# Moving a few VectorE and ScalarE instructions within the pair phases of a macaron transformer block

## The chip, the cores and the metric

The kernel runs on one core of a Trainium2 chip. The metric is the device time of one launch in microseconds (us). TensorE (PE in the profile, PEld for its weight loads) multiplies, VectorE (DVE) and ScalarE (ACT) prepare operands and empty its banks, GpSimd (POOL) and SyncE (SP) issue transfers. Each engine works through its own list in order; semaphores tie the lists together.

## The reference

A block of 512 positions by 1024 features in float32: half a SwiGLU layer, a token mixer, half a SwiGLU layer, a norm.

```python
def swiglu(x, w_gate, w_up, w_down):
    return (jax.nn.silu(x @ w_gate) * (x @ w_up)) @ w_down

x = x + 0.5 * swiglu(rmsnorm(x, ffn1_norm[layer]), ...)
x = x + token_mixer(rmsnorm(x, mix_norm[layer]), ...)
x = x + 0.5 * swiglu(rmsnorm(x, ffn2_norm[layer]), ...)
return rmsnorm(x, final_norm)
```

The hidden width of a SwiGLU layer is 2816, that is 22 tiles of 128.

## The kernel before, in words

**Products in two parts.** Every float32 operand is split into a high part (a rounding cast, by ScalarE) and a low part (operand minus high part, by VectorE). A product is then three matmuls into one PSUM bank: high by high, high by low, low by high (`mm3`, L124 to L126).

**Plain and pair phases.** In each SwiGLU layer (function `ffn`, called with the suffix "a" for the first and "b" for the second) some hidden tiles are computed plainly with matmuls 512 wide. The rest go in pairs of hidden tiles by a scheme of Strassen's kind, with seven products of half width (256 columns) in place of eight. A *unit* is one such set of seven: `("g", j)` is the gate of tiles j and j+1, `("u", j)` their up projection, `("d", group, m)` the down projection onto features m and m+1. `("p", m)` is a plain down product between them. The list `units` sets their order: the first gate, then g and u in turn, then p and d. There are 23 pair units in the first layer and 25 in the second, 336 steps in all.

**A step.** `SEVEN` gives the seven steps of a unit, each one product of 4 by 3 matmuls into one of four banks W, X, Y, Z:

```python
SEVEN = (("a11", "w", "b11"), ("s3", "z", "t3"), ("s2", "x", "t2"), ("a12", "w", "b21"),
         ("s1", "y", "t1"), ("a22", "x", "t4"), ("s4", "y", "b22"))
```

After a11 ScalarE copies W's bank to X's, as a seed onto which s2 adds; after s2 it copies X's to Y's, onto which s1 adds. After s3 it copies Z's bank to SBUF (`p7`, kept in `rbc_n` for a gate and in `sq` for an up unit). After s1 VectorE adds Y's bank and `p7` (L415 in a gate or up unit, `rbc_n<-pyga`) or updates `x` from it (L424 in a down unit, `x<-pyda`); only then may s4 go on adding into Y's bank. After a22 the same is done for X's bank.

**What sets the order.** TensorE's order is written out. For VectorE and ScalarE a heap of events does it: `at(time, rank, f)` puts a call at a planned time, calls of one time come out by rank and then in the order in which they were put; `put` is `at` with rank 0. The planned times are on a grid of `STEP`, one product each; they only order the lists. For the product that begins at `starts[t]`, `total` (the sum s2 or s4, L365 and L367) is made 5 steps ahead, `high` (the cast of its weights, L383) 4 steps ahead at rank 3, and `low` (L387) 3 steps ahead at rank 2.5. In `pair_step` `silu` (L477) turns a gate's W, p7 and Y parts into `g0` and `g1`. In `kept` the activated pair is split again for the down products: `t0_parts` (L557) casts T0 and `t0_rest` (L527) makes its low part. In the last group of down units of the first layer `to_mixer` also scales and casts each finished `x` (L798) and squares it for the norm (L791, L794).

Of the kernel before, what the change touches and what calls it, by code (L numbers as in the profile page):

```python
# [22 lines left out]
S = 512  # L23
# [31 lines left out]
STEP, PLAIN_STEP = 1410, 4080  # L55
# [10 lines left out]
def tile_macaron(ctx: ExitStack, tc, xs, xT, wf, wgu1, wst1, wd1, wdg1, wqk, wv, wo, wgu2, wst2, wd2,  # L66
                 wdg2, lams, relb, onehot, addc, out):
    nc = tc.nc
    V, A, G, T = nc.vector, nc.scalar, nc.gpsimd, nc.tensor
# [24 lines left out]
    x = [None] + [cp.tile([P, S], F32, tag=f"x{k}", name=f"x{k}")[:] for k in range(1, KD)]  # L94
# [104 lines left out]
    def ffn(wgu, wst, wd, wdg, n0, n1, norm, early, res, nm, hooks, ended, first=None,  # L199
# [91 lines left out]
        left, right = slice(0, HS), slice(HS, S)  # L291
# [11 lines left out]
        ops, begin, starts, now = [], {}, [], 0  # L303
# [98 lines left out]
        def at(time, rank, f, *a):  # L402
            count[0] += 1
            heapq.heappush(events, (time, rank, count[0], f, a))

        def put(time, f, *a):
            at(time, 0, f, *a)
# [18 lines left out]
        def product(t):  # L426
            u, o = ops[t]
            h, l = made.pop(t)
            if o[0] == "p":
                m = u[1]  # L430
                po = mm_bank(f"pd{nm}{m}")
                for k in range(PLAIN):
                    c = slice(k * P, (k + 1) * P)
                    mm3(po[:], h[:, c], l[:, c], ah[k][:], al[k][:], k == 0, k == PLAIN - 1)
                put(starts[t + 1], stt, x[m], po[:], 0.5, x[m], ALU.add)
                return
            if t == begin[u]:
                made[u] = {}
                for b, tag in zip("wxyz", bank_tags(u)):
                    made[u][b] = pp.tile([P, S], F32, tag=tag, name=f"p{b}{u[0]}{nm}{t}",  # L440
                                         bufs=4 if tag == "mm" else 2)[:, :HS]
            banks = made[u]
            seeded = o[0] not in ("a11", "s3")
            if t == 0 or ops[t - 1][1][0] == "p":
                T.matmul(banks[o[1]][:, :P], h[:, :P], moving(u, o[2])[0][0][:, :P],
                         start=True, stop=False, skip_group_check=True)
            for p, mv in enumerate(moving(u, o[2])):
                c = slice(p * P, (p + 1) * P)
                mm3(banks[o[1]], h[:, c], l[:, c], *mv, not seeded and p == 0, p == 3, seeded)


            if o[0] == "a11":
                put(starts[t + 1], A.copy, banks["x"], banks["w"])
            elif o[0] == "s2":
                put(starts[t + 1], A.copy, banks["y"], banks["x"])
            elif u[0] == "d":
                down_step(starts[t + 1], u, o[0], banks)
            else:
                pair_step(starts[t + 1], u, o[0], banks)
# [8 lines left out]
        def pair_step(t, u, o, banks):  # L468
            j = u[1]
            pw, px, py, pz = (banks[b] for b in "wxyz")  # L470
            p7 = (sq if u[0] == "u" else res["bc"])[:, left]

            def silu(r, c, p, scale=1.0):

                if r not in g.setdefault(j, {}):
                    g[j][r] = tp.tile([P, S], F32, tag="ptb", name=f"g{r}{nm}{j}")
                A.activation(g[j][r][:, c], p, AF.Silu, scale=scale)  # L477

            def times_up(r, c):
                mul(g[j][r][:, c], ups[j + r][:, c], g[j][r][:, c])  # L480

            if o == "s3":
                put(t, A.copy, p7, pz)
            elif u[0] == "g":


                if o == "a12":
                    if j == n1:
                        put(t, silu, 0, left, pw)
                        put(t + STEP, times_up, 0, left)  # L490
                    else:
                        at(t + STEP, 2, silu, 0, left, pw)
                elif o == "s1":
                    put(t, add, res["bc"][:, right], py, p7)
                elif o == "a22":
                    put(t, add, p7, px, p7)
                    put(t + STEP * (j > n1), silu, 1, slice(0, S), res["bc"][:], -1.0)
                elif o == "s4":
                    put(t, silu, 0, right, py)
                    if j == n1:  # L500
                        put(t, times_up, 1, slice(0, S))
                        put(t + STEP, times_up, 0, right)
                        kept(j, t, t - 2 * STEP, t + STEP)
            else:
                g0, g1 = g[j][0], g[j][1]
                if o == "a12":
                    put(t, mul, g0[:, left], pw, g0[:, left])
                elif o == "s1":
                    put(t, add, sq[:, right], py, p7)
                elif o == "a22":  # L510
                    put(t, add, sq[:, left], px, p7)
                    put(t, stt, g1[:], sq[:], -1.0, g1[:], ALU.mult)
                elif o == "s4":
                    put(t, mul, g0[:, right], py, g0[:, right])
                    kept(j, t - STEP, t - 3 * STEP, t)

        def kept(j, t1, t0, t2):

            g0, g1 = g[j][0], g[j][1]

            def cast(o, a):
                A.copy(o, a)

            def rest(o, a, h):
                V.tensor_tensor(o, a, h.bitcast(F32), op=ALU.subtract)  # L527

            def parts(t, h, l, a):
                put(t, cast, h, a)  # L530
                put(t + STEP, rest, l, a, h)

            if j < PLAIN:
                for r, t in ((1, t1), (0, t2)):
                    h = ah[j + r] = slot(j + r, f"ah{nm}{j + r}", F32R)
                    l = al[j + r] = slot(JF + j + r, f"al{nm}{j + r}", F32R)
                    parts(t + STEP, h[:], l[:], g[j][r][:])
                return
            places = [lambda n=n, i=i: slot(i, f"h{n}{nm}{j}", F32R)
                      for n, i in enumerate(PAIR_SLOTS[(j - PLAIN) // 2 % 4])]  # L540
            t = {}

            def b11():
                t["b"] = places[0]()
                A.copy(t["b"][:, left], g0[:, left])

            def b2():
                t["h2"] = places[1]()
                A.copy(t["h2"][:], g1[:])

            def b2_rest():
                t["l2"] = places[2]()
                rest(t["l2"][:], g1[:], t["h2"][:])

            def t0_parts():
                t["h0"] = places[3]()
                A.copy(t["h0"][:], g0[:])  # L557

            def t0_rest():
                t["l0"] = places[4]()  # L560
                rest(t["l0"][:], g0[:], t["h0"][:])

            def t1_parts():
                t["h1"] = places[5]()
                A.copy(t["h1"][:], g1[:])

            def t1_rest():
                t["l1"] = places[6]()
                rest(t["l1"][:], g1[:], t["h1"][:])
                b = hs[j] = {"b11": (t["b"][:, left], t["b"][:, right])}  # L570
                for n, i, c in (("b21", 2, left), ("b22", 2, right), ("t1", 0, left),
                                ("t3", 0, right), ("t4", 1, left), ("t2", 1, right)):
                    b[n] = t[f"h{i}"][:, c], t[f"l{i}"][:, c]

            put(t0 + STEP, b11)
            put(t0 + 2 * STEP, lambda: rest(t["b"][:, right], g0[:, left], t["b"][:, left]))
            put(t1 + STEP, b2)
            n = max(t1, t2)
            put(n, less, g0[:, left], g0[:, left], g0[:, right])
            put(n + STEP, b2_rest)  # L580
            put(n + STEP, less, g0[:, right], g1[:, right], g0[:, right])
            put(n + 2 * STEP, t0_parts)
            put(n + 2 * STEP, stt, g1[:, right], g1[:, right], -1.0, g0[:, left], ALU.subtract)
            put(n + 2 * STEP, stt, g1[:, left], g1[:, right], -1.0, g1[:, left], ALU.subtract)

            at(n + 3 * STEP, 5, t1_parts)
            late = 2 * STEP * (j > n1)
            at(n + 3 * STEP + late, 1, t0_rest)
            at(n + 4 * STEP + late, 1, t1_rest)
# [23 lines left out]
        def pipeline():  # L613
            seen = {}
            for t, (u, o) in enumerate(ops):
# [4 lines left out]
                else:  # L620
# [13 lines left out]
                    if o[0] in ("s2", "s4"):  # L634
                        at(starts[t] - 5 * STEP, 2, total, t)
                    at(starts[t] - 4 * STEP, 3, high, t)
                    at(starts[t] - 3 * STEP, 2.5, low, t)
                at(starts[t], 4, product, t)
            if bias is not None:
                at(starts[begin["p", 5]], 5, bias[0])  # L640
# [23 lines left out]
        for j in range(j0, n1):  # L664
# [9 lines left out]
            for hf in range(2):  # L674
                wh, wl = get_w(wgu[j, hf], f"gu{nm}{j}_{hf}")
                for kk in range(4):
                    k = hf * 4 + kk
                    for c, pt in ((0, pg), (1, pu)):
                        o = kk * 256 + c * P
# [34 lines left out]
    with tc.manual_schedule(engines={mybir.EngineType.DVE, mybir.EngineType.Activation}):  # L714
        for t in range(4):
            raw = wp.tile([P, 1024], F32, tag="raw", name=f"raw_f{t}")
            h, l = w_place()
            for kk in range(2):
# [18 lines left out]
                for j in range(2):  # L737
                    for c in range(2):
                        o = kk * 512 + (2 * j + c) * P
# [37 lines left out]
    n1 = {}  # L777
# [55 lines left out]
    at = {}  # L833
# [536 lines left out]
```

## Time and profile before

| what | us |
|---|---|
| three runs: lowest, median, highest | 935.04, 937.92, 938.45 |
| the profiled execution, its device time | 934.85 |
| span of the profiled execution, first to last instruction | 933.1 |
| PE busy in it | 916.4 (98%) |
| VectorE, ScalarE, GpSimd busy in it | 723.9, 532.0, 98.3 |

All durations below come from the profiled execution; its own time is 1.8 us over its span. In the timeline's rows the first number is the start in us from the span's start, the second the duration, and in square brackets stands how long the engine sat idle before it and who ended that. A 256-wide matmul's row is longer than the distance to the next one, since matmuls are pipelined; what counts is the distance from start to start.

### The profile page before, as it was taken

How to read it: one execution, taken by the hardware profiler on the slowest of the kernel's cores; microseconds unless marked ns; L12 is line 12 of the kernel's file. 1: busy time of each engine (PE TensorE's matmuls, PEld its weight loads, DVE VectorE, ACT ScalarE, POOL GpSimd, SP SyncE). 2: the span in 40 equal slices, each digit the busy share in tenths (PEclk: the TensorE clock that was granted, in tenths of full speed). 3: DMA queues.
4: the chain of work that ended last, by engine and by line, in shares of the span. 5: the costliest groups of instructions: out<-in, count | busy, mean ns of one | idle time of the engine just before them, and what ended most of it. 6: DMA issues, size and time to landing. Idle time of an engine off the chain costs nothing.

```text
span 933.1 us, 17213 instructions
## 1 busy us (share of the span) xinstructions
PE 916.4 (98%) x6462; PEld 848.4 (91%) x6462; DVE 723.9 (78%) x1490; ACT 532.0 (57%) x1102; POOL 98.3 (11%) x117
## 2 busy tenths in 40 slices
PE   9999999999999999999999999999999999999995
PEld 7788999999999998988989888888999899999995
DVE  6697897687997896668764537597899778798786
ACT  7455664355664665566756645355666445666462
POOL 0011101112102100000000002201110102220100
PEclk9999999999999999999999999999999999999997
DMA  7176646578757641443333103345775667874832
GB/s 251 65 194 157 167 127 176 137 195 223 195 150 193 188 128 65 131 136 113 91 113 92 68 23 117 121 136 142 177 171 137 175 168 178 216 215 124 209 103 91
DMA packets 60388, 136.71 MB, mean 147 GB/s; under 512 B 6848, under 2 KB 9152, under 8 KB 60304
## 3 DMA queue, kind: packets, MB, share of 16 engines
q1 hardware_dynamic: 46304, 110.14, 35.8%
q0 software_dynamic: 14000, 25.47, 17.4%
q8 instruction: 50, 0.82, 0.4%
q14 instruction: 34, 0.28, 0.1%
HBM read 130.30 MB, written 2.14 MB: 142 GB/s over the span
## 4 chain that ended last, share of the span: by engine, by line
PE 91%; DVE 6%; ACT 2%; issue 1%; DMA 1%; SPq 0%; DVEq 0%
PE po L1039 3%; PE pwo L124 1%; PE pwo L125 1%; PE pwo L126 1%; PE pua L126 1%; PE pua L125 1%; PE pua L124 1%; PE pv L896 1%; PE pv L897 1%; PE pv L898 1%; PE pt L1026 1%; PE pq L124 1%; PE pq L126 1%; PE pq L125 1%; PE pdb L124 1%; PE pda L124 1%
## 5 line engine op out<-in xcount | busy, mean ns | idle before, releaser
L1005 DVE CUSTOM_DVE_ANT_0 pr<-sc,strip 128x128 f32<-128x128 f32 (+3 forms) x64 | 30.9, 488 | 34.8 <-PE sc L1003 34.2
L1008 ACT ACTIVATE pr<-pr,small 128x128 f32<-128x128 f32 (+3 forms) x64 | 36.0, 563 | 32.1 <-DVE small L1005 31.2
L383 ACT CAST w<-s2b 128x512 fp32r<-128x512 f32 x50 | 31.1, 622 | 14.1 <-DVE s2b L365 12.7
L383 ACT CAST w<-s2a 128x512 fp32r<-128x512 f32 x46 | 28.7, 623 | 15.9 <-DVE s2a L365 13.3
L151 POOL TENSOR_TENSOR sq<-sq,sqt 128x512 f32<-128x512 f32 x7 | 10.9, 1559 | 254.4 <-ACT sqt L150 254.4
L387 DVE TENSOR_TENSOR w<-s2b,w 128x512 fp32r<-128x512 f32 x50 | 34.3, 686 | 4.3 <-ACT w L383 4.3
L1039 PEld LDWEIGHTS po<-v,ptb 128*128 128x128 f32 x240 | 32.7, 191 | 5.3 <-ACT ptb L1029 2.7
L896 PE MATMUL pv<-w,xh 128*128 128x256 f32 x128 | 35.9, 281 | 0.0
L897 PE MATMUL pv<-w,xl 128*128 128x256 f32 x128 | 35.8, 280 | 0.0
L898 PE MATMUL pv<-w,xh 128*128 128x256 f32 x128 | 35.7, 279 | 0.0
L387 DVE TENSOR_TENSOR w<-s2a,w 128x512 fp32r<-128x512 f32 x46 | 31.5, 686 | 3.9 <-ACT w L383 3.9
L1039 PE MATMUL po<-v,ptb 128*128 128x64 f32 (+1 forms) x240 | 32.5, 269 | 1.8 <-ACT ptb L1029 1.7
L1029 ACT COPY ptb<-pt 128x128 f32<-128x128 f32 (+3 forms) x48 | 20.0, 424 | 20.2 <-PE pt L1026 19.9
L124 PE MATMUL pq<-xh,w 128*128 128x512 f32 x64 | 26.9, 421 | 0.0
L124 PE MATMUL pwo<-mh,w 128*128 128x512 f32 x64 | 26.1, 407 | 0.0
L125 PE MATMUL pwo<-ml,w 128*128 128x512 f32 x64 | 25.5, 399 | 0.0
L126 PE MATMUL pwo<-mh,w 128*128 128x512 f32 x64 | 25.5, 398 | 0.0
L124 PE MATMUL pk<-xh,w 128*128 128x512 f32 x64 | 25.1, 393 | 0.0
L125 PE MATMUL pq<-xl,w 128*128 128x512 f32 x64 | 25.1, 392 | 0.0
L126 PE MATMUL pq<-xh,w 128*128 128x512 f32 x64 | 25.1, 392 | 0.0
L126 PE MATMUL pk<-xh,w 128*128 128x512 f32 x64 | 25.0, 391 | 0.0
L125 PE MATMUL pk<-xl,w 128*128 128x512 f32 x64 | 25.0, 390 | 0.0
(671 smaller groups left out, 3973.8 us busy)
## 6 DMA issues: line engine op xcount, KB each, us to landing
raw_qk<-wqk_dram SPq DMA_DIRECT2D x16, 512.0 KB, 3.5
raw0bg<-wst_dram SPq DMA_DIRECT2D x9, 512.0 KB, 4.6
raw_gua<-wgu_dram SPq DMA_DIRECT2D x8, 512.0 KB, 3.9
raw0ag<-wst_dram SPq DMA_DIRECT2D x8, 512.0 KB, 4.8
raw0ad<-wdg_dram SPq DMA_DIRECT2D x8, 512.0 KB, 5.0
strip<-bias_rows SPq DMA_DIRECT2D x16, 256.0 KB, 3.5
raw_v<-wv_dram SPq DMA_DIRECT2D x8, 512.0 KB, 3.2
raw_wo<-wo_dram SPq DMA_DIRECT2D x8, 512.0 KB, 3.2
```

The source lines that it names most:

```text
L124: T.matmul(po, wh, mh, start=first, stop=False, skip_group_check=on)
L125: T.matmul(po, wh, ml, start=False, stop=False, skip_group_check=on)
L126: T.matmul(po, wl, mh, start=False, stop=last, skip_group_check=on)
L383: A.copy(made[t][0], source(t))
L387: V.tensor_tensor(l, source(t), h.bitcast(F32), op=ALU.subtract)
L896: T.matmul(po, xh[k][:, xs], wh[:, o:o + 256], start=k == 0, stop=False)
L897: T.matmul(po, xl[k][:, xs], wh[:, o:o + 256], start=False, stop=False)
L898: T.matmul(po, xh[k][:, xs], wl[:, o:o + 256], start=False, stop=k == KD - 1)
L1005: V.tensor_tensor_reduce(out=pi, in0=ps[:, :w], in1=st["b"][m][:, w - 1::-1], op0=ALU.add, op1=ALU.min, scale=1.0, scalar=3.0e38, accum_ou ...
L1008: A.activation(pi, pi, AF.Exp, scale=-1.0, bias=st["mx"][:, m, i:i + 1], accum_out=st["ls"][:, m, i:i + 1])
L1029: A.copy(ptb[:, :w], pt[:, :w])
L1039: T.matmul(st["po3"][:, i, d0:d0 + dn], st["ptb", m, i][:, k * P:(k + 1) * P], vt[u // 4, k][:, fo + d0:fo + d0 + dn], start=k == 0, stop= ...
```

## The change

Four things move, all within the lists of VectorE and ScalarE; TensorE's, GpSimd's and SyncE's lists are the same instructions in the same order.

- The low part of the weights for a11 is put two steps ahead at rank 0.5, where it was three steps ahead at rank 2.5, unless a plain product stands before that a11. So it comes after the instruction that empties Y's bank of the unit before. This is done for 42 of the 48 units.
- The two seed copies get rank -1, and so come before all else of their time.
- `silu` of W's part gets rank 3.5 and so comes after the cast of the same time; `silu` of p7's part is put a step later (not in a layer's first gate).
- T0's cast gets rank 0.5, behind the copies.

```diff
             if o[0] == "a11":
-                put(starts[t + 1], A.copy, banks["x"], banks["w"])
+                at(starts[t + 1], -1, A.copy, banks["x"], banks["w"])
             elif o[0] == "s2":
-                put(starts[t + 1], A.copy, banks["y"], banks["x"])
+                at(starts[t + 1], -1, A.copy, banks["y"], banks["x"])
...
                     else:
-                        at(t + STEP, 2, silu, 0, left, pw)
+                        at(t + STEP, 3.5, silu, 0, left, pw)
...
-                    put(t + STEP * (j > n1), silu, 1, slice(0, S), res["bc"][:], -1.0)
+                    put(t + 2 * STEP * (j > n1), silu, 1, slice(0, S), res["bc"][:], -1.0)
...
-            put(n + 2 * STEP, t0_parts)
+            at(n + 2 * STEP, 0.5, t0_parts)
...
                     at(starts[t] - 4 * STEP, 3, high, t)
-                    at(starts[t] - 3 * STEP, 2.5, low, t)
+                    if o[0] == "a11" and t and ops[t - 1][1][0] != "p":
+                        at(starts[t] - 2 * STEP, 0.5, low, t)
+                    else:
+                        at(starts[t] - 3 * STEP, 2.5, low, t)
```

VectorE in the second gate of the first layer, before, where `raw0au` is the weight tile whose low part the up unit's a11 needs and `pyga` is the gate's bank Y:

```order
L365 TENSOR_TENSOR s2a_1018<-s1au_800,raw0au 128x512
L387 TENSOR_TENSOR w<-raw0au,w 128x512
L415 TENSOR_TENSOR rbc_n_373<-pyga_945,rbc_n_373 128x256
L527 TENSOR_TENSOR h6a_1037<-g1a_910,h5a_1034 128x512
L387 TENSOR_TENSOR w<-s3au_803,w 128x512
```

The same place now:

```order
L365 TENSOR_TENSOR s2a_1018<-s1au_800,raw0au 128x512
L415 TENSOR_TENSOR rbc_n_373<-pyga_945,rbc_n_373 128x256
L387 TENSOR_TENSOR w<-raw0au,w 128x512
L527 TENSOR_TENSOR h6a_1037<-g1a_910,h5a_1033 128x512
L387 TENSOR_TENSOR w<-s3au_803,w 128x512
```

The low part and the add that empties Y's bank have changed places; nothing else has.

ScalarE in the same gate, before, where `h3a` is T0's cast, `pyga<-pxga` the seed of Y's bank and `g0a`, `g1a` the silus:

```order
L557 CAST h3a_997<-g0a_875 128x512
L412 COPY pyga_945<-pxga_944 128x256
L383 CAST w<-raw0au 128x512
L383 CAST w<-s3au_803 128x512
L565 CAST h5a_1034<-g1a_910 128x512
L477 ACTIVATE g0a_1039<-pwga_943 128x256
L383 CAST w<-s2a_1018 128x512
L383 CAST w<-raw0au 128x512
L477 ACTIVATE g1a_1070<-rbc_n_373 128x512
L477 ACTIVATE g0a_1039<-pyga_945 128x256
L383 CAST w<-s1au_800 128x512
L412 COPY pxua_1086<-pwua_1085 128x256
```

And now:

```order
L412 COPY pyga_945<-pxga_944 128x256
L557 CAST h3a_1000<-g0a_875 128x512
L383 CAST w<-raw0au 128x512
L383 CAST w<-s3au_803 128x512
L565 CAST h5a_1033<-g1a_910 128x512
L383 CAST w<-s2a_1018 128x512
L477 ACTIVATE g0a_1041<-pwga_943 128x256
L383 CAST w<-raw0au 128x512
L477 ACTIVATE g0a_1041<-pyga_945 128x256
L383 CAST w<-s1au_800 128x512
L412 COPY pxua_1084<-pwua_1083 128x256
L477 ACTIVATE g1a_1100<-rbc_n_373 128x512
```

The seed has gone ahead of T0's cast, the first silu one place down, the silu of p7's part three places down, behind the up unit's first seed.

ScalarE in the last group of the first layer's down units, both in one (- before, + now; the lines of the mixer's calls are numbered 3 higher in the changed file):

```order
 L383 CAST w<-s1ad_6_3647 128x512
-L798 ACTIVATE xh_82<-x_100,x_104 128x512
-L791 ACTIVATE sqd_3929<-x_100 128x512
 L412 COPY pxda_3911<-pwda_3910 128x256
+L801 ACTIVATE xh_82<-x_100,x_104 128x512
+L794 ACTIVATE sqd_3930<-x_100 128x512
 L383 CAST w<-raw1ad 128x512
 L412 COPY rbc_n_373<-pzda_3913 128x256
```

Here the seed of X's bank has gone ahead of the mixer's scaled cast and square of an `x`.

## The prediction

> **What bounds the kernel now.** First the page: the share of each engine and the chain that ended last.
>
> ```profile
> PE 916.4 (98%) x6462; PEld 848.4 (91%) x6462; DVE 723.9 (78%) x1490; ACT 532.0 (57%) x1102; POOL 98.3 (11%) x117
> PE 91%; DVE 6%; ACT 2%; issue 1%; DMA 1%; SPq 0%; DVEq 0%
> ```
>
> TensorE works 916.4 of 933.1 us and the chain is 91% TensorE. The change leaves its instructions alone, so it can only give back time in which TensorE waits. The view of who waited for whom, for PE, shows how little stands at the instructions that move (us in total, times, longest):
>
> ```profile
> PE bc_n L193 <- DVE dg_n L189: 0.8, 2, 0.5
> ...
> PE pyda L124 <- DVE x L424: 0.4, 1, 0.4
> PE pyga L124 <- DVE rbc_n L415: 0.3, 1, 0.3
> ```
>
> That view misses short lateness, because a matmul's row lasts longer than its turn. So I read starts instead. Here are the first matmuls of two following steps, and the windows view of PE over two stretches of 10.08 us of pair steps (its x counts every matmul with a part in the stretch).
>
> ```profile
> 106.56 0.28 PE L124 MATMUL pzua<-txa,w 128*128 128x256 f32 x1
> ...
> 107.92 0.28 PE L124 MATMUL pxua<-txa,w 128*128 128x256 f32 x1
> 106.56:116.64 10.08, 10.08 (x91) 1.00 0.78 194
> 143.42:153.50 10.08, 10.08 (x86) 1.00 0.46 140
> ```
>
> A step is 1.36 us, so 113 ns a matmul. 10.08/0.1133 is 89 starts; the two matmuls still under way at the left edge make 91. I take this as the floor. The second stretch starts 84, one per 120 ns, at the same granted clock of 1.00: TensorE has slipped into a slower cadence there and stays in it. A slip costs 0.08 us a step. The question is what starts one.
>
> **The edge.** At the end of every gate unit VectorE's add of Y's bank must end before s4's first weight load. Rows of three gates, VectorE and PEld:
>
> ```profile
> 141.41 0.41 DVE L415 TENSOR_TENSOR rbc_n<-pyga,rbc_n 128x256 f32<-128x256 f32 x1
> 141.88 0.19 PEld L124 LDWEIGHTS pyga<-xh,w 128*128 128x128 f32 x1
> 238.18 0.68 DVE L387 TENSOR_TENSOR w<-raw0au,w 128x512 fp32r<-128x512 f32 x1
> 238.78 0.41 DVE L415 TENSOR_TENSOR rbc_n<-pyga,rbc_n 128x256 f32<-128x256 f32 x1
> 239.12 0.68 DVE L527 TENSOR_TENSOR h4a<-g0a,h3a 128x512 fp32r<-128x512 f32 x1
> 239.25 0.19 PEld L124 LDWEIGHTS pyga<-xh,w 128*128 128x128 f32 x1
> 240.72 0.28 PE L124 MATMUL pwua<-xh,w 128*128 128x256 f32 x1
> 855.86 0.42 DVE L415 TENSOR_TENSOR rbc_n<-pygb,rbc_n 128x256 f32<-128x256 f32 x1
> 856.33 0.19 PEld L124 LDWEIGHTS pygb<-xh,w 128*128 128x128 f32 x1
> ```
>
> In all three the load begins some 0.05 us after the add ended (141.82, 239.19, 856.28): it is released by the add, just in time. At 141.88 it was a few ns too late, and that is where the slip of the stretch above began. The gates between them have the same lists, so I take most to run on this edge, in both layers. With the low part behind the add, the add starts where the low part started, 0.60 us earlier (238.18 for 238.78), and the edge is gone. The low part moves back by 0.34 (238.78 to 239.12) and ends at 239.20 instead of 238.86; its product starts at 240.72, so 1.5 us of cover remain, and without that cover it would cost what it overshoots.
>
> **The change part by part.** *The slip at 142.* 7 steps at 0.08, and the start of it, come back: 0.6 us, with 0 to 0.7 as bounds, since a slip could start elsewhere.
>
> *The first gate pair of the first layer.* ScalarE's seed, VectorE's add, and the two places where TensorE waits for them:
>
> ```profile
> 92.47 0.68 DVE L387 TENSOR_TENSOR w<-s3ag,w 128x512 fp32r<-128x512 f32 x1
> 93.48 0.42 DVE L415 TENSOR_TENSOR rbc_n<-pxga,rbc_n 128x256 f32<-128x256 f32 x1 [0.33 <-PE pxga L126]
> 99.42 0.62 ACT L557 CAST h3a<-g0a 128x512 fp32r<-128x512 f32 x1 [0.90 <-DVE g0a L421]
> 99.95 0.36 ACT L412 COPY pyga<-pxga 128x256 f32<-128x256 f32 x1
> 99.97 0.28 PE L126 MATMUL pwga<-xh,w 128*128 128x256 f32 x1
> 100.36 0.39 PE L124 MATMUL pyga<-txa,w 128*128 128x256 f32 x1
> 103.10 0.28 PE L126 MATMUL pxga<-tta,w 128*128 128x256 f32 x1
> 103.23 0.42 DVE L415 TENSOR_TENSOR rbc_n<-pyga,rbc_n 128x256 f32<-128x256 f32 x1
> 103.71 0.39 PE L124 MATMUL pyga<-xh,w 128*128 128x256 f32 x1 [0.33 <-DVE rbc_n L415]
> ```
>
> TensorE starts Y's s1 0.39 after the matmul before it instead of 0.11 (0.28 lost), and s4 0.61 after (0.50 lost). The seed waited behind T0's cast, which waited 0.90 for VectorE; moved ahead, it starts when s2 is done and the first loss goes. That alone gains nothing at the exit, since s4 waits for the add anyway. The add starts 0.60 earlier by the trade. But VectorE already loses 0.19 at 92: there the low part now lies behind the add, pushes the row at 92.47 back by 0.60, and its end passes the start at 93.48 by about 0.19, and VectorE has no idle time from there to here. So s4 starts 0.60 - 0.19 = 0.4 us earlier. Bounds 0 and 0.8.
>
> *The down units before the mixer.* Here PE waits for VectorE and for ScalarE's seed; the windows view shows a slip to the end.
>
> ```profile
> 321.50 0.42 DVE L424 SCALAR_TENSOR_TENSOR x<-pyda,x 128x256 f32<-128x256 f32 x1 [0.22 <-PE pyda L126]
> 329.40 0.28 PE L126 MATMUL pxda<-h5a,w 128*128 128x256 f32 x1
> 330.06 0.39 PE L124 MATMUL pyda<-h1a,w 128*128 128x256 f32 x1 [0.38 <-DVE x L424]
> 331.74 0.42 DVE L424 SCALAR_TENSOR_TENSOR x<-pyda,x 128x256 f32<-128x256 f32 x1 [0.20 <-PE pyda L126]
> 333.77 0.36 ACT L412 COPY pxda<-pwda 128x256 f32<-128x256 f32 x1
> 334.26 0.32 PE L124 MATMUL pxda<-h5a,w 128*128 128x256 f32 x1
> 334.42 0.28 PE L125 MATMUL pxda<-h6a,w 128*128 128x256 f32 x1
> 335.74:341.50 5.76, 5.76 (x51) 1.00 0.48 177
> 351.14 1.12 PE L193 MATMUL bc_n<-dg_n,ones_m 128*128 128x512 f32 x2 [0.34 <-DVE dg_n L189]
> ```
>
> TensorE loses 0.55 at 330.06, 0.05 at 334.42 and some 0.25 in the slip after it (51 where the floor has 53): about 0.9 in all. The trade and the seed's place remove these. What is late next is VectorE: it makes the norm's factors that TensorE waits for at 351.14 and is busy without a break but for the 0.22 and 0.20 above. It can come earlier by those only, so 0.4 us passes and the rest lengthens the wait at 351.14 from 0.34 to about 0.8. Bounds 0 and 0.9. The mixer's cast and square now lie behind the seed, so they come later by its 0.36 and by its wait for a11. VectorE reads them further down its list, which hides it: nothing; uncovered it would be about 0.4 in each of the three units.
>
> *The silus and T0's cast elsewhere.* No wait of PE names them; they are read by the up unit's VectorE work, a unit later: nothing, bounds 0 and 0. No DMA moves and no queue of SP or POOL is passed.
>
> Sum: 0.6 + 0.4 + 0.4 = 1.4 us; 934.85 - 1.4 = 933.4 for a run like the profiled one.
>
> **Where this stands to the median.** The median, 937.92, is 3.07 above the profiled execution, for a reason that no view of it shows. An edge that is missed by nanoseconds in one gate and met in the next would differ between executions; four more long slips like the 0.6 us above would make 2.4. I credit half of the 3.07 to such slips, 1.5, as a choice between 0 and all: 937.92 - 1.4 - 1.5 = 935.0.
>
> [...] The wait at 351.14 grows, and a longer one had a sequel:
>
> ```profile
> 535.94 0.32 PE L1039 MATMUL po<-v,ptb 128*128 128x64 f32 x1 [1.69 <-ACT ptb L1029]
> 537.18:540.59 3.41, 3.41 (x12) 0.50 0.31 96
> ```
>
> After 1.69 us idle the granted clock was 0.50 for 3.41 us, which costs half of it, 1.7 us. A wait of 0.8 lies between this and the 0.38 at 330.06, after which the clock was still 1.00 at 335.74; it is nearer to the latter, so I take no drop and keep 1.7 for the range. [...]
>
> **The rivals.**
>
> *All of the spread was edges* (0.20). If the 3.07 is all slips and TensorE's 0.9 in the down units passes whole: 937.92 - 3.07 - 1.9 = 932.9. For it: the edge is at nanoseconds. Against: VectorE binds at 351.14.
>
> *Nothing passes* (0.15). Slips return elsewhere, or the clock drops: 935.0 + 1.7 = 936.7, up to 937.9. This is also the case that the change does not do what it says: most gates lose nothing today.
>
> *A slip in most units* (0.06), the slower one. The low part of a11 becomes the late one: 42 units have it nearer to its product, and if it ended after that product's first load in half of them, 21 units of 7 steps at 0.08 make 11.8: 937.92 + 11.8 - 1.4 = 948.3. It decides from the point where the low part's end comes within 0.05 us of the load. Against it: the 1.5 us of cover.
>
> *The floor is none* (0.01). [...]
>
> **How the numbers follow.** The forecast has 0.58: between 933.4 and 936.5 (all or none of the 3.07), predicted 935.0. A measurement of this kernel tells 0.5% from no change, 4.7 us: below 933.2 is faster, above 942.6 slower. The rival of edges falls below, with 0.01 for the floor: faster 0.21. The slower rival gives 0.06, and 0.73 is left for the same. The range takes in the forecast, the edges' case and the one where nothing passes: 932.0 to 938.0.
>
> **What would show it.** Right: in the changed trace the adds L415 end 0.6 us or more before s4's first load in every gate; steps of 1.36 throughout 98 to 153; no wait of PE for L415 or L424; the wait at L193 before the mixer longer than 0.34. Wrong: the first gate pair still waits 0.3 or more for L415, a slip starts at an up unit's a11 or s3, or the clock falls after L193. The prediction fails outright if the time is over 942 or under 932.

## The result and the profile after

| what | before, us | after, us |
|---|---|---|
| median (lowest to highest) of 21 runs each, side by side | 937.40 (932.95 to 941.67) | 934.15 (930.67 to 935.76) |
| profiled execution, its device time | 934.85 | 933.51 |
| its span | 933.1 | 931.7 |

The ratio is 0.9963, 95% interval 0.9949 to 0.9977: 0.4% faster, and within the 0.5% that was called no change. The forecast of 935.0 and its range held. The profiled executions differ by 1.34 us, the medians by 3.25; so here too more than half of the difference lies between executions and not in the one that was profiled.

The page of the changed kernel, the shares and the chain, and then the view of who waited for whom, for PE (us in total, times, longest):

```profile
PE 915.7 (98%) x6462; PEld 847.8 (91%) x6462; DVE 722.5 (78%) x1490; ACT 533.8 (57%) x1102; POOL 98.2 (11%) x117
PE 88%; DVE 7%; ACT 2%; issue 1%; DMA 1%; SPq 0%; DVEq 0%
```

```profile
PE pga L124 <- ACT w L115: 1.0, 2, 0.8
PE bc_n L193 <- DVE dg_n L189: 0.8, 2, 0.5
...
PE pyga L124 <- DVE rbc_n L415: 0.2, 1, 0.2
PE pyda L124 <- DVE x L424: 0.2, 1, 0.2
```

Both waits of the pair phases are still there, at about half their size. The first row is the kernel's start-up, 0.3 us longer than before.

The gate that the prediction showed at 238 us, in the timeline of the changed kernel (VectorE, PEld, PE):

```profile
237.33 0.69 DVE L365 TENSOR_TENSOR s2a<-s1au,raw0au 128x512 f32<-128x512 f32 x1
237.93 0.42 DVE L415 TENSOR_TENSOR rbc_n<-pyga,rbc_n 128x256 f32<-128x256 f32 x1
238.26 0.69 DVE L387 TENSOR_TENSOR w<-raw0au,w 128x512 fp32r<-128x512 f32 x1
238.82 0.19 PEld L124 LDWEIGHTS pyga<-xh,w 128*128 128x128 f32 x1
240.29 0.28 PE L124 MATMUL pwua<-xh,w 128*128 128x256 f32 x1
```

The add now ends at 238.35, 0.47 before the load, where 0.06 was left before. It is not the full 0.6, since TensorE comes 0.43 earlier at this place and VectorE 0.25. The low part ends at 238.95, 1.34 before its product.

The same distance, from the add's end to s4's first load, over all 17 gates: before, it was 0.05 to 0.06 in twelve of them and 0.63 in the other five. Now it is 0.45 to 0.48 in eleven of the twelve and unchanged in the five. The twelfth, with 0.05 as before, is the first gate pair.

The first gate pair (ScalarE's seed and cast, VectorE's add, and where PE waits):

```profile
99.81 0.36 ACT L412 COPY pyga<-pxga 128x256 f32<-128x256 f32 x1 [0.30 <-PE pxga L126]
100.43 0.62 ACT L557 CAST h3a<-g0a 128x512 fp32r<-128x512 f32 x1 [0.26 <-DVE g0a L421]
100.81 0.28 PE L126 MATMUL pwga<-xh,w 128*128 128x256 f32 x1
100.92 0.28 PE L124 MATMUL pyga<-txa,w 128*128 128x256 f32 x1
102.31 0.69 DVE L527 TENSOR_TENSOR h4a<-g0a,h3a 128x512 fp32r<-128x512 f32 x1
102.92 0.68 DVE L365 TENSOR_TENSOR s2a<-s1au,raw0au 128x512 f32<-128x512 f32 x1
103.52 0.42 DVE L415 TENSOR_TENSOR rbc_n<-pyga,rbc_n 128x256 f32<-128x256 f32 x1
103.99 0.39 PE L124 MATMUL pyga<-xh,w 128*128 128x256 f32 x1 [0.19 <-DVE rbc_n L415]
```

The seed is off the path: Y's first matmul comes 0.11 after the one before it, where it was 0.39. The add is still late. T0's low part (102.31) still stands ahead of it here, while in the other gates it stands behind it.

The last of the down units before the mixer, and the norm's first matmul behind them:

```profile
338.57 0.42 DVE L424 SCALAR_TENSOR_TENSOR x<-pyda,x 128x256 f32<-128x256 f32 x1
339.05 0.38 PE L124 MATMUL pyda<-h1a,w 128*128 128x256 f32 x1 [0.15 <-DVE x L424]
350.15 1.12 PE L193 MATMUL bc_n<-dg_n,ones_m 128*128 128x512 f32 x2 [0.34 <-DVE dg_n L189]
```

The unit before this one lost 0.55 at 330.06 and now loses 0.13; this one, the last, waits instead, and the wait at L193 has its old 0.34.

**By place.** I took the start of the same matmul in both traces at several landmarks; a table gives how far the changed kernel is behind (+) or ahead (-), and what that makes of each stretch.

| landmark (us in before) | after minus before | the stretch up to it |
|---|---|---|
| 27.99, first norm | +0.85 | start-up +0.85 |
| 105.20, a11 of the first up unit | +0.28 | first gate pair -0.57 |
| 173.93, end of the first gates and ups | -0.43 | slip at 142 -0.71 |
| 321.30 | -0.56 | -0.13 |
| 335.74, a12 of the last down unit | -1.26 | down units -0.70 |
| 341.50, mixer | -0.99 | rest of the last down unit +0.27 |
| 590.40, second layer | -0.90 | mixer +0.09 |
| end of the span | -1.34 | second layer and end -0.44 |

So between these two executions 2.2 us came back behind the start-up, and this execution's start-up, which the change does not touch, took 0.85 of it.

For the experiments I use one more measure, the *excess*: for every pair step, the time from its first matmul to the next step's first, less 1.36 us (less 1.507 for the six steps that carry a thirteenth matmul), summed. It was 4.45 us in before and 2.27 in after. Every kernel was timed beside runs of before on the same chip; kernels that share such runs form one group of four or fewer, and medians are compared within a group.

### The profile page after: what moved, and what is told of

It is laid out like the page before. It is cut to its first block, busy times and chain, and to the rows that moved or that the text cites. A ratio compares the mean times of both kernels' runs of the same rounds, so it can differ in the third digit from the quotient of the medians.

```text
span 931.7 us, 17210 instructions
## 1 busy us (share of the span) xinstructions
PE 915.7 (98%) x6462; PEld 847.8 (91%) x6462; DVE 722.5 (78%) x1490; ACT 533.8 (57%) x1102; POOL 98.2 (11%) x117
## 4 chain that ended last, share of the span: by engine, by line
PE 88%; DVE 7%; ACT 2%; issue 1%; DMA 1%; SPq 0%; DVEq 0%
PE po L1042 3%; PE pwo L124 1%; PE pwo L125 1%; PE pwo L126 1%; PE pua L126 1%; PE pua L125 1%; PE pua L124 1%; PE pv L899 1%; PE pv L900 1%; PE pv L901 1%; PE pt L1029 1%; PE pq L124 1%; PE pq L126 1%; PE pq L125 1%; PE pda L124 1%
```

## The experiments

Theory: what is gained comes from the low part's new place, by gates that stand on the edge; the seeds matter in the first pair and the down units; the silus matter nowhere. Rivals: ScalarE's moves carry it; or the gain is chance.

### The kernel before, once more

No edit: a second profile.

> A second profiled execution of the kernel before, nothing edited. Theory of the edges: the gates run so close to the edge that which of them slip differs between executions. So the steps longer than 1.36 us stand at other gates than 122.88 and 141.98, their sum differs from the first profile's by 0.5 us or more, and that sum explains most of the difference in time. Rival: the same steps are long by the same amounts within 0.1 us, and a different time comes from elsewhere (the start, the mixer, the clock).

935.33 us, span 933.5, excess 6.90. The first row is from the view of the timeline, the others from the windows view of PE:

```profile
103.23 0.39 PE L124 MATMUL pyga<-xh,w 128*128 128x256 f32 x1 [0.31 <-DVE rbc_n L415]
```

```profile
106.56:116.64 10.08, 10.08 (x86) 1.00 0.75 185
120.00:134.00 14.00, 14.00 (x119) 1.00 0.71 185
143.42:153.50 10.08, 10.08 (x87) 1.00 0.42 132
```

In the first execution the stretch from 106.56 held 91 matmuls, here 86: the slip began at the first pair's late add and lasted until the plain phase at 155, 36 steps at 0.08, or 2.8 us. The same wait at the same place (0.33 in the first) was not followed by a slip there. So slips do differ between executions, as the prediction supposed; but the largest one hangs on the first pair's wait and not on a gate's edge. It was expected that the excess explains most of the difference in time, and it does not: it is 2.45 more, and the execution only 0.48 us longer, since 1.5 us were saved in the mixer (see the clock below) and 0.4 in the start-up.

### The parts alone

The low part's move without ScalarE's (e_low: before, with the last hunk of the diff), ScalarE's moves without the low part's (e_act: after, without that hunk), and the low part's move in the second layer alone:

```diff
 # e_low_b, against before
+if nm == "b" and o[0] == "a11" and t and ops[t - 1][1][0] != "p":
+    at(starts[t] - 2 * STEP, 0.5, low, t)
+else:
     at(starts[t] - 3 * STEP, 2.5, low, t)
```

> Only the low part of a11's weights goes behind the add that empties Y's bank; ScalarE's list is that of before. Theory of the edges: nearly the whole gain, a ratio of 0.9955 to 0.9975 against the kernel before, and times that spread less than those of before; in the profile every gate's add ends 0.5 us or more before s4's first load. Rival (seeds and silus carry it): a ratio of 0.9985 or more, since the seeds' waits in the first pair and in the down units stay.

> Only ScalarE's moves (seeds first, silus and T0's cast later); VectorE's list is that of before. Theory of the edges: the gates stay on their edge, a ratio of 0.999 to 1.000 and a spread as wide as before; in the first pair the seed's wait of 0.28 is gone from the profile and the wait for L415 is longer by as much. Rival (seeds and silus carry it): a ratio of 0.9975 or less.

> The low part moves in the second SwiGLU layer alone, where the first profile of before shows no step of a gate longer than 1.38 us; everything else is that of before. Theory of the edges: other executions do slip there, so the median falls by 0.7 to 2 us (a ratio of 0.998 to 0.9993) although that profile has nothing to give back. Rival (the profile's stalls are all there is): a ratio of 1.000 within 0.0005.

| kernel | median (12 runs) | ratio to before (933.88 beside them) | excess |
|---|---|---|---|
| e_low | 932.15 | 0.9984 (0.9973 to 0.9996) | 3.50 |
| e_act | 934.10 | 1.0005 (0.9992 to 1.0018) | 3.98 |
| e_low_b | 934.04 | 0.9999 (0.9987 to 1.0011) | 3.87 |

The low part's move alone is worth 1.5 us, ScalarE's moves alone nothing that can be told. The 0.9955 to 0.9975 expected of e_low was not reached; 0.9984 lies at the edge of the rival's range. The second layer's gates by themselves gave nothing either: the interval leaves at most 1.2 us either way. These runs of before had a median only 1.7 us over its lowest run.

But the low part alone doesn't do what the whole change does. The up unit behind the same gate, in e_low's timeline (ScalarE's seed of X, PEld, and two matmuls of PE that should start 0.34 apart), and then in after's:

```profile
241.94 0.38 ACT L412 COPY pxua<-pwua 128x256 f32<-128x256 f32 x1
242.37 0.19 PEld L124 LDWEIGHTS pxua<-txa,w 128*128 128x128 f32 x1
242.47 0.29 PE L124 MATMUL pxua<-txa,w 128*128 128x256 f32 x1
242.83 0.28 PE L124 MATMUL pxua<-txa,w 128*128 128x256 f32 x1
```

```profile
241.85 0.36 ACT L412 COPY pxua<-pwua 128x256 f32<-128x256 f32 x1 [0.47 <-PE pwua L126]
242.90 0.19 PEld L124 LDWEIGHTS pxua<-txa,w 128*128 128x128 f32 x1
```

In e_low the seed ends at 242.32 and the load starts 0.05 later: TensorE got ahead, and the edge passed from VectorE's add to ScalarE's seed, which lay behind two silus and a cast. That step took 1.410 us. In after one of the silus lies behind the seed, which ends 0.69 before the load.

e_low_b has the same long steps, 1.40 to 1.41 us at the seed of X in six up units of the second layer. Their excess in that layer's gates and ups is 0.29 us, where the two profiles of before have 0.02 and 0.25. So e_low_b put another edge in the place of the first, and its 0.9999 doesn't tell what the gates' edges cost there.

### The change less one of its parts

After again, after with the seeds and T0's cast where they were (low_silu), and after with the silus where they were (low_seed):

```diff
 # low_silu, against after
-                at(starts[t + 1], -1, A.copy, banks["x"], banks["w"])
+                put(starts[t + 1], A.copy, banks["x"], banks["w"])
...
-                at(starts[t + 1], -1, A.copy, banks["y"], banks["x"])
+                put(starts[t + 1], A.copy, banks["y"], banks["x"])
...
-            at(n + 2 * STEP, 0.5, t0_parts)
+            put(n + 2 * STEP, t0_parts)
 # low_seed, against after
-                        at(t + STEP, 3.5, silu, 0, left, pw)
+                        at(t + STEP, 2, silu, 0, left, pw)
...
-                    put(t + 2 * STEP * (j > n1), silu, 1, slice(0, S), res["bc"][:], -1.0)
+                    put(t + STEP * (j > n1), silu, 1, slice(0, S), res["bc"][:], -1.0)
```

> The changed kernel again, with a second profile, beside its parts. If the slips of a whole stretch (120 ns a matmul for several us) are what differs between executions, its profile has none of more than two steps before the mixer, and its time stands below the low part alone (0.9984 against before): 0.996 to 0.998. Rival (the low part is all of it): 0.9984 and no better.

> The low part's move and the two silus' moves; seeds and T0's cast stay where they were. Theory (the low part alone handed the edge to the up unit's first seed, pxua<-pwua, because ScalarE has a silu in front of it): the steps of pxua and pxub, 1.38 to 1.41 us with the low part alone, are 1.36 in every unit, the first pair's wait for Y's seed stays at 0.4 to 0.5, and the down units before the mixer still lose at X's seed. Rival (the seeds' rank cures it): the steps of pxua and pxub stay above 1.36 in most units.

> The low part's move, seeds first and T0's cast behind them; the silus stay where they were. Theory (the silus hold the up unit's seed): the steps of pxua and pxub stay 1.37 to 1.41 in most units, while the first pair loses no more than 0.5 in all and X's seed in the down units before the mixer is never waited for. Rival: 1.36 at pxua and pxub, and a time equal to the whole change.

| kernel | median (12 runs) | ratio to before (935.35 beside them) | excess: first pair and short losses in the gates behind it, long slip there, down units, all |
|---|---|---|---|
| after_2 | 932.60 | 0.9972 (0.9958 to 0.9985) | 0.54, 2.80, 0.75, 5.15 |
| low_silu | 931.86 | 0.9961 (0.9946 to 0.9975) | 0.58, 0, 0.90, 2.54 |
| low_seed | 932.53 | 0.9970 (0.9956 to 0.9983) | 0.54, 2.80, 0.73, 5.59 |

For comparison, before has 1.10, 0.65, 1.29 and 4.45 in these columns, e_low 0.63, 0, 1.37 and 3.50, e_act 1.05, 0, 1.27 and 3.98. The three times are one within their intervals, so neither ScalarE part can be told from nothing by the times once the low part has moved. By the traces the first pair is the low part's, and the silus guard the up units, as was expected: where it isn't slipping, low_seed has the steps of X's seed in the up units at 1.40 to 1.42 us, and low_silu has them all at 1.36. In the down units the low part together with either ScalarE move has less excess than the low part or ScalarE's moves alone; but that is one profile each, and 1.1 of e_low's 1.37 there is a slip of 14 steps.

The changed kernel itself slipped from the first pair on in its second profile, against what was expected of after_2. Timeline and windows of PE:

```profile
102.53 0.39 PE L124 MATMUL pyga<-xh,w 128*128 128x256 f32 x1 [0.19 <-DVE rbc_n L415]
```

```profile
120.00:134.00 14.00, 14.00 (x119) 1.00 0.67 171
```

The wait is 0.19 as in the first profile of after, in which that stretch holds 126 matmuls. The change makes this wait shorter, and a slip starts from it or doesn't. So I took the wait away.

### The first pair mended

In a layer's first gate the low parts of T0 and T1 are put a step later, as in its other gates, so that T0's comes behind the add (best_first). In `best` the loading of the square root's table is also moved, from s3 to a12 of the very last unit, so that it comes behind the seed of Y, which waited for it. best_2 is best once more:

```diff
 # best_first, against after
-            late = 2 * STEP * (j > n1)
+            late = STEP * (1 + (j > n1))
...
 # best: also
+        if o == "a12":
+            put(t, A.activation, root[:], eps[:], AF.Sqrt)
...
-        if o == "s3":
-            put(t, A.activation, root[:], eps[:], AF.Sqrt)
-        elif o == "s1":
+        if o == "s1":
```

> The changed kernel with two more moves: in the first gate pair the low parts of T0 and T1 are made a step later, behind the add of Y's bank (VectorE has no idle time there), and at the end ScalarE's table load for the last root comes after Y's seed instead of before it. Theory (what is left in those two places is order alone): the wait for L415 of 0.2 to 0.35 near 104 and the wait for Y's seed of 0.3 near 913 go, 0.6 to 0.8 us in all, a ratio 0.0006 to 0.0009 below the changed kernel. Rival (absorbed by the next wait, as before the mixer): less than 0.3 us.

> The changed kernel with both more moves, again, for a second profile and more times. Theory (a long slip of some 36 steps starts only from the late add of the first gate pair, which this kernel no longer has): no step before 157 is longer than 1.37 us, and the times spread over less than 4 us, where the changed kernel spreads over 5. Rival (long slips come from anywhere): a long slip stands before 157 in this profile, or the times spread as widely.

> The changed kernel with the first gate pair's move alone; ScalarE's table load stays before the last Y seed. Theory (the first pair is where most of what is left lay, by its wait of 0.5 and by the long slip of 2.8 that follows it in some executions): a ratio within 0.0005 of the kernel with both moves, and 0.3 us at the wait for Y's seed near 912 stays in its profile. Rival (the table load is what the better time came from): the time of the changed kernel.

| kernel | median (lowest to highest, runs) | ratio to before, beside it |
|---|---|---|
| best | 931.43 (930.03 to 932.42, 6) | 0.9957 (0.9943 to 0.9971) |
| best_2 | 931.55 (930.03 to 934.32, 9) | 0.9913 (0.9885 to 0.9942) |
| best_first | 930.35 (929.82 to 932.46, 7) | 0.9915 (0.9883 to 0.9947) |

Before's medians were 935.35 and 937.60. The new kernels have the lowest medians of this study. best stands 1.2 us under after_2, run beside it, but their intervals overlap, and low_silu is within 0.5 us of best; so a gain in time over the change is not shown. best_first, with its one line, is as quick as best_2, so the table's move is not seen in the times.

The 1.2 us between the medians of those two go with something else, the granted clock. Of the 14 profiled executions nine have a mean granted clock of 0.993 or less, and all nine have a drop of the clock in the mixer (see below). Three have 0.995 or more and no drop; of the two at 0.994 one has it. best_first's five runs at 0.995 took 929.82 to 930.58 us and its two at 0.993 931.64 and 932.46. best_2's two at 0.995 took 930.03 and 930.04 and its six at 0.993 931.41 to 934.32. So a good part of what still differs between executions here goes with the mean clock, and by the profiles with that drop; best_first had the lower clock less often.

In best VectorE's order at the first pair, and the windows of PE:

```profile
101.78 0.42 DVE L415 TENSOR_TENSOR rbc_n<-pyga,rbc_n 128x256 f32<-128x256 f32 x1
102.12 0.68 DVE L387 TENSOR_TENSOR w<-raw0au,w 128x512 fp32r<-128x512 f32 x1
102.72 0.69 DVE L527 TENSOR_TENSOR h4a<-g0a,h3a 128x512 fp32r<-128x512 f32 x1
```

```profile
120.00:134.00 14.00, 14.00 (x126) 1.00 0.60 155
```

The add ends at 102.20 and s4's first matmul starts at 102.50, with no wait. By the traces the gain is as expected: an excess of 1.46 in best and 1.82 in best_first, where after has 2.27. In none of the three profiles was there a slip in this phase. My theory, that with this wait the long slips would be gone, fell all the same with best_2. ScalarE and PEld at the first gate behind the plain phase of the second layer, and the windows of PE from there on within the pair phase, first of best_2 and then of best:

```profile
811.10 0.63 ACT L557 CAST h3b<-g0b 128x512 fp32r<-128x512 f32 x1 [0.71 <-DVE g0b L421]
811.76 0.63 ACT L383 CAST w<-s2b 128x512 fp32r<-128x512 f32 x1
812.28 0.37 ACT L412 COPY pygb<-pxgb 128x256 f32<-128x256 f32 x1
812.70 0.19 PEld L124 LDWEIGHTS pygb<-txb,w 128*128 128x128 f32 x1 [0.20 <-ACT pygb L412]
813.00:864.00 51.00, 51.00 (x427) 1.00 0.66 169
```

```profile
812.25 0.37 ACT L412 COPY pygb<-pxgb 128x256 f32<-128x256 f32 x1
812.93 0.19 PEld L124 LDWEIGHTS pygb<-txb,w 128*128 128x128 f32 x1
813.00:864.00 51.00, 51.00 (x452) 1.00 0.69 180
```

In both, T0's cast and the total's cast lie ahead of Y's seed, and the seed starts at the same time within 0.03. In best_2 TensorE gets there first, the load waits, and the slow cadence begins and stays: with two matmuls under way at the left edge, 425 start in 51 us, one per 120 ns, and in best 450, one per 113. In best TensorE reached this place later and the seed was in time. The excess of this phase is 3.31 us in best_2 and 0 in best, and best_2's profiled run is its slowest; its times spread over 4.3 us, where less than 4 was expected. So a long slip can start at other waits too, and a kernel whose TensorE runs ahead meets others. What decides whether a given wait starts one is not settled.

### The add one instruction later

Before, with VectorE's add of Y's bank put later, which brings it behind T0's or T1's low part in 12 gates:

```diff
-                    put(t, add, res["bc"][:, right], py, p7)
+                    at(t, 1.5, add, res["bc"][:, right], py, p7)
```

> The kernel before with the opposite move: in the gate units the add of Y's bank goes one instruction further back, behind the low part of T0 or T1, in 12 of the 17 gates. Theory of the edges (the add ends 0.05 us before s4's first load is due, no cover): each of these gates loses nearly the whole 0.60 us of that instruction and some 0.1 at the restart, 12 x 0.55 to 0.7, so 6.5 to 8.5 us and a ratio of 1.007 to 1.009. Rival (there is cover that the profile does not show): under 3 us, a ratio below 1.003.

942.68 us (940.96 to 944.96, 10 runs), ratio 1.0035 (1.0006 to 1.0065), excess 12.74. The same gate (VectorE, PEld):

```profile
239.22 0.68 DVE L387 TENSOR_TENSOR w<-raw0au,w 128x512 fp32r<-128x512 f32 x1
239.83 0.68 DVE L527 TENSOR_TENSOR h4a<-g0a,h3a 128x512 fp32r<-128x512 f32 x1
240.43 0.41 DVE L415 TENSOR_TENSOR rbc_n<-pyga,rbc_n 128x256 f32<-128x256 f32 x1
240.90 0.19 PEld L124 LDWEIGHTS pyga<-xh,w 128*128 128x128 f32 x1 [0.82 <-DVE rbc_n L415]
```

The load follows the add's end by 0.06, as in the prediction's rows, and the step ahead of s4 takes 2.15 us for 1.36. By the profile this is 8.3 us more excess than before's, and the profiled run's 943.09 is 8.2 over before's 934.85. The mechanism is thus shown at its price, inside the 6.5 to 8.5 us expected: the add is the one that s4 waits for. The ratio is under the 1.007 expected, because before's own runs went from 932.15 to 945.51 in the runs beside it, while edge_late's stayed within 4 us: with the add late in every execution there may be little left to differ. That suggests, and does not show, that before's spread is lateness that is met in some executions and missed in others. The clock's drop is not its main source: at a mean granted clock of 0.995 or more 13 of before's 27 runs there still went from 932.15 to 944.18. But no profile holds one of the long executions, whose times are those of edge_late and more, so where they lose up to 10 us stays open. Before's lowest run was nearly the same in all four groups (932.95, 932.18, 932.28, 932.15), while its median went from 933.88 to 937.60.

### Less work for VectorE in the down units

In after the last down unit waits for VectorE. Here best, with the add of the norm's squares on GpSimd:

```diff
-        put(t + 2 * STEP, lambda: V.tensor_tensor(sq[:], sq[:], sqt[0][:], op=ALU.add))
+        put(t + 2 * STEP, lambda: E.tensor_tensor(sq[:], sq[:], sqt[0][:], op=ALU.add))
...
-        squared(m, t, put)
+        squared(m, t, put, G)
```

> The kernel with both more moves, and in the first layer's last down units the seven sums of squares for the norm (0.60 us each on VectorE) go to GpSimd. Theory (VectorE, busy without a break, is what TensorE waits for there and at L193): the waits of 0.7 us in these down units go and the wait at L193 shrinks, 0.7 to 1.5 us, a ratio 0.0007 to 0.0016 below the kernel without it. Rival (GpSimd's add, 1.56 us each by the rows of its squares in the plain phase, or its transfers' issues come late): the norm's factors are later and the time is the same or longer.

935.13 us, ratio 0.9964 (0.9939 to 0.9989), where best_2 has 0.9913 beside it: 3.6 us slower, as the rival had it. GpSimd, VectorE and PE in its timeline, and the windows of PE behind the wait:

```profile
332.65 1.66 POOL L798 TENSOR_TENSOR sq<-sq,sqd 128x512 f32<-128x512 f32 x1 [0.66 <-ACT sqd L795]
333.07 1.79 DVE L387 TENSOR_TENSOR w<-s1ad,w 128x512 fp32r<-128x512 f32 x1
339.71 0.38 PE L124 MATMUL pyda<-h1a,w 128*128 128x256 f32 x1 [2.01 <-DVE x L424]
340.42:343.83 3.41, 3.41 (x14) 0.50 0.65 221
```

VectorE's low part, 0.68 elsewhere, took 1.79 here: it started 0.42 after GpSimd's add had begun and ended 0.55 after that was done. So by these rows it got little of its 0.68 done in the 1.24 us that the two share; why, no run shows. Behind it, with no add of GpSimd's under them, the low parts at 335.44 and 336.71 took 0.68 again. Five rows of VectorE in these units took 1.35 to 1.82 us in this way, so it lost more than the adds had cost it, and the down units' excess rose from 0.73 to 4.14. Of that some 0.7 belong to the clock, an estimate: behind the wait of 2.01 it was 0.50 for 3.41 us, and at 113 ns a start about six matmuls of s4 are left for that window, each some 113 ns longer at half the clock.

## Why the prediction was right, and where it was not

**The slip at 142** (forecast 0.6): 0.71 in the landmarks. The stretch that held 86 matmuls holds 89, the windows view of PE in after shows:

```profile
143.42:153.50 10.08, 10.08 (x89) 1.00 0.49 139
```

The size was right, but in part by luck. VectorE's order at that gate is still the old one in e_act and e_low_b, and their steps there are 1.38 and 1.37 with no slip behind them. So an execution can miss this slip without the change; what the change shows is that the add no longer stands on the edge there (0.46).

**The first gate pair** (0.4): 0.57. The mechanism was as told, the seed free and the add half as late; the term was mis-sized by 0.17. VectorE's loss of 0.19 at 92 came (0.17 at the add of X's bank, start-up left out), but it did not last: before, the low part at 100.82 started 0.46 behind the row ahead of it, and now, at 101.71, 0.34 behind. There was a short wait in VectorE's list where the prediction had "no idle time", and it took up 0.12 of the loss.

**The down units** (0.4 of 0.9 to pass): 0.47 by the second layer's start. The size was right, the reason only half so. By the excess before lost 1.29 there and not 0.9: the prediction left out the step of 1.49 at 319.81 and most of the slow matmuls behind its two waits. The prediction had TensorE run free through these units and the rest appear as a longer wait at L193, 0.8. That wait kept its 0.34, and the rest stands in the last down unit, where s4 waits for L424 (339.05): 0.27 given back. VectorE has no idle time there, as the prediction said; the step that failed is which of its results is late first.

**The silus and T0's cast: nothing.** This step failed in its reason. By the times they are nothing, but e_low and low_seed show what they hold off: with the low part moved alone TensorE comes up to the seed of X within 0.05 us, and the steps there take 1.38 to 1.42. No wait in the trace of before named them because the edge had not yet passed to them.

**The median** (1.5 of 3.07 credited to slips at the gates' edges). The medians fell by 1.9 more than the profiled executions, so the size was near, but by luck: 1.5 was a choice between 0 and all. No run shows that the gates' edges make up the spread, and the one slip of several us that was seen in before (2.8) starts at the first pair's wait, which the change leaves at half its size and which slipped in after too. What is shown is that slips of 2.8 us (before_2, after_2), a drop of the clock and the start-up differ between executions; what makes most of before's spread stays open.

**Not foreseen:** the end of the second layer came 0.44 earlier, by the low part's move: the last down units have an excess of 1.19 in before and e_act and of 0.82 in e_low. And start-up came 0.85 later in this execution; best's start-up is 0.30 earlier than before's, so it differs by execution.

**The adds** were to end 0.6 before s4's load in every gate, and the kernel to hold steps of 1.36 from 98 to 153. It was some 0.47 in eleven gates and 0.05 in the first pair; one step, at 102.28, took 1.71, and in after_2 and low_seed every step from the first pair's s4 on took 1.44. **The slower rival** (a slip in most units) did not come: the low part ends some 1.34 before its product in eleven gates and 0.94 in the first pair. **Nothing passes** is excluded by the ratio. **All spread was edges** is not quite: after's medians were 934.15, between its 932.9 and the forecast, and 932.60, though beside a before of 935.35.

**The clock.** No drop followed the norm's wait in after: behind the 0.34 at L193 the granted clock was 1.00 from 350.15 to 353.60. The window of 0.50 behind the 1.69 wait at 536 is there in 10 of the 14 profiles of this study and not in the other four, with the same wait. The timeline of before's second profile, and its window as long behind that wait as the prediction's was:

```profile
537.78 1.10 PE L1039 MATMUL po<-v,ptb 128*128 128x64 f32 x8 [1.70 <-ACT ptb L1029]
539.02:542.43 3.41, 3.41 (x21) 1.00 0.32 94
```

The clock stayed at 1.00, and 21 matmuls have a part in the window where 12 had. Between the mixer's start and the second layer's, that execution gained 1.5 us on the first profile; so the 1.7 that the prediction put in its range is about what a drop costs. Waits of TensorE of up to 0.93 us in the pair phases (edge_late) were followed by no drop, and the one of 2.01 in best_g was. What decides whether the wait of 1.7 is followed by it, no run shows.

**The floor** (0.01 that it is none): 1.36 a step stood in every profile, and none went under it: the shortest of the 336 steps took 1.360 us in before and 1.359 in after, 113 ns a matmul. No run shows a shorter turn.

## What to carry to other kernels

When an engine that paces a kernel is released just in time, look at how many hundredths lie between the last release and the load that needs it, at every place and for every releaser: here moving the low part alone moved the edge from VectorE's add to ScalarE's seed (0.05 us in e_low), and no wait in the trace of before had named that one. Mend the first wait of a phase first, since a slow cadence that begins there can last until the phase's end (36 steps in before_2, 2.8 us); here one line at the first pair took that wait away, and none of the four profiles without it had a slip in that phase, while the changed kernel slipped there in one of its two. And compare medians only between runs made side by side where the kernel's own executions differ: the lowest time of before stayed while its median moved by 3.7 us.

## What the runs showed of the hardware

After a late weight load TensorE may keep starting matmuls 120 ns apart instead of 113, at a granted clock of 1.00: for 36 steps, 2.8 us, in before_2, and in best_2 for all of the 51 us from 813 on. Most of these slips lasted until the phase changed; the one in e_low's down units ended inside a unit after 14 steps. The length of the wait doesn't decide it: at the first pair's s4 waits of 0.31, 0.19 and 0.19 us started a slip (before_2, after_2, low_seed), and waits of 0.33, 0.19, 0.72, 0.34 and 0.93 did not (before, after, e_act, e_low_b, edge_late). In edge_late the cadence was 118 ns (steps of 1.413) twice for a dozen steps.

From the end of the instruction that releases it, the first weight load starts 0.05 to 0.06 us later, on VectorE's and ScalarE's results alike. The row of its matmul began 0.10 behind the load's at 242.47 in e_low, and 0.01 behind it at 103.71 in before.
